# A delta-net stage: weight tiles split at unit five of the preceding tile, raw weights given out two tiles ahead

## The chip, the core and the metric

The kernel runs on one core of a Trainium2 chip. Its time is the device time of one execution in microseconds (us); the time of a kernel is the median of several runs. Five engines work side by side, each through its own queue in order: TensorE (PE in the profile, with its weight loads as PEld) multiplies matrices, VectorE (DVE), ScalarE (ACT) and GpSimd (POOL) work elementwise, SyncE (SP) issues most of the DMA transfers here. They wait for one another by semaphores.

## The reference, cut to what matters

A sequence of 1024 tokens with 1024 features goes through two residual layers. The first is a gated delta net (chunks of 64 in the reference, heads of 128) and a convolutional feed-forward part, the second a banded attention with another feed-forward part. All of it is float32. The stage that matters here is the delta net:

```python
proj = xn @ w_in                                  # 1024 x 4112
qkv = silu(causal_dwconv(proj[..., :3072], conv_w))
z = proj[..., 3072:4096]
q, k = l2norm(q) * 128 ** -0.5, l2norm(k)
o = chunk_gated_delta_rule(q, k, v, beta, g)      # a recurrence over chunks, 8 heads
o = rmsnorm(o, out_norm_w) * silu(z)
h = x + o @ w_out
```

## The kernel before

**Products in two halves.** Every float32 matrix product is made from rounded parts: an activation is split into `xh` (rounded) and `xl` (the rest), a weight tile into `whi` and `wlo`. `dense` (line 114) issues three matmuls for each of the eight k-slices: `whi` by `xh` (L120), `whi` by `xl` (L121), `wlo` by `xh` (L122). One such triple of 128 x 512 matmuls is called a unit here.

**Weight tiles.** The input projection has 32 weight tiles of 1024 x 128: eight each for k, q, v and the gate z. A tile has 16 units: eight for the first half of the sequence (half 0), eight for the second (half 1), each half ending in `post`. The raw tile (512 KB) is loaded by SP into `wraw` (L575; two buffers), cast on ScalarE to `whi` (L103, 128 x 1024) and subtracted on GpSimd in four pieces to `wlo` (L105, 128 x 256 each). `whi` and `wlo` have two buffers each. A generator `dense_tile` has these steps: issue the load, yield, split, yield, then the units. The last two z tiles share a generator `last_tiles`, which issues both loads at once and runs half 0 of both before half 1. After the input projection come 16 tiles of the output projection (`out_tile`, eight units each, loads on L1249).

**What follows a half tile.** `project.post` takes the accumulator through ScalarE (L615, L617), three VectorE taps of the short convolution (L625), a tanh on ScalarE (L630) and two GpSimd operations (L631, L632). For half 0 of k and q the result stays in `kq` and TensorE reads it there (L660 transposes q, L717 multiplies k by itself); the results of half 1 of k and q and both halves of v are stored to DRAM (line 635) and fetched later. The recurrence itself (`gram`, `invert_blocks`, `merge`, `prep`, `chain`, `output`, `finish`) is made of many short matmuls of 128 columns or fewer between operations of VectorE and ScalarE, and its loads and stores all go through SP: `at` (L748), `eq` (L750), `vv` (L766), the stores of d_m, d_u, d_e, d_y, d_z.

**What sets the order.** `Flow` is a planner that runs while the program is being written. It keeps a planned time `T`: a unit costs 0.69 us (line 292), each recurrence step has a fixed cost, and `on` keeps the planned busy time of VectorE, ScalarE and GpSimd. `run` emits the recurrence step of the highest rank whose inputs are due, else the next unit. The order thus written is binding for TensorE, VectorE and ScalarE (`manual_schedule`, line 1305). The order on GpSimd's and SP's queues is made afterwards, instruction by instruction, from what is ready first.

**The queue of tiles in the planner.** `nxt` holds tiles whose load has been emitted: one, or two when `brief` is set (line 262). From a tile's second unit on, `_dense` calls `fetch` after each unit (line 294). `fetch` first fills `nxt`, which emits loads, and then emits the split of the first entry, if the current tile has reached `split_at` units and six planned microseconds have passed since that entry's load was emitted (line 268). `split_at` comes with the current tile: 8, or what its generator yields after its split (26 in `last_tiles`, 1 in `out_tile`). `brief` is set in `last_tiles`, so the output tiles run with two entries. The six lines:

```python
while len(self.nxt) < (2 if self.brief else 1):
    ...
    self.nxt.append([e[2], 1, self.T, e[1], 8])
if split and self.nxt and self.nxt[0][1] == 1 and (split > 1 or self.T >= self.nxt[0][2] + 6.0):
    self.nxt[0][1] = 2
    self.nxt[0][4] = next(self.nxt[0][0]) or 8
```

A second `Flow` plans the attention stage (line 1973), with its own `brief` at line 2313.

Of the kernel before, what the change touches and what calls it, by code (L numbers as in the profile page):

```python
# [28 lines left out]
def trunk_kernel(  # L29
# [52 lines left out]
    def act_tiles(halves=(0, 1), into=None):  # L82

        xh, xl = into or ([[None, None] for _ in range(KT)], [[None, None] for _ in range(KT)])
        for k in range(KT):
            for s in halves:
                xh[k][s] = actp.tile([P, HALF], F32R, name=f"xh{k}_{s}", tag=f"xh{k}_{s}")
                xl[k][s] = actp.tile([P, HALF], F32R, name=f"xl{k}_{s}", tag=f"xl{k}_{s}")
        return xh, xl
# [39 lines left out]
    class Weave:  # L129
# [3 lines left out]
        def __init__(self):  # L133
            self.dense, self.short, self.solve, self.late = deque(), deque(), deque(), deque()
            self.now, self.credit, self.turn, self.budget = 0, 0.0, 0.0, 0.0
            self.at = {}
# [63 lines left out]
    class Flow(Weave):  # L200
# [4 lines left out]
        def __init__(self):  # L205
            super().__init__()
            self.T, self.free, self.aux = 0.0, dict(D=0.0, A=0.0, G=0.0), deque([[0.0], [0.0]])
            self.time, self.items, self.last, self.stalls = {}, [], 0, []
            self.auto, self.tick, self.slack, self.cur, self.nxt, self.units = True, 0, 0.5, None, deque(), 0
            self.brief, self.split_at, self.hold = False, 8, None  # L210

        def mark(self, key, t=None):
            super().mark(key)
# [46 lines left out]
        def fetch(self, split):  # L260

            while len(self.nxt) < (2 if self.brief else 1):
                e = self.pick()
                if e is None:
                    break
                next(e[2])
                self.nxt.append([e[2], 1, self.T, e[1], 8])
            if split and self.nxt and self.nxt[0][1] == 1 and (split > 1 or self.T >= self.nxt[0][2] + 6.0):
                self.nxt[0][1] = 2
                self.nxt[0][4] = next(self.nxt[0][0]) or 8  # L270

        def _dense(self):
            if self.cur is None:
# [128 lines left out]
    wv = None  # L402
# [107 lines left out]
    with ExitStack() as ph:  # L510
# [48 lines left out]
        def units(s, wt, post):  # L559

            ps = pacc.tile([P, HALF], F32, name="acc", tag="acc", bufs=3)
            for i in range(KT):
                dense(ps, wt, 0, xh, xl, FULL[i : i + 1], s, first=i == 0, last=i == KT - 1)
                if i < KT - 1:
                    yield
            post(s, ps)
            tiles[s] += 1
            if tiles[s] == 30:
                act_tiles((s,), acts)
                wv.mark(("acts", s))  # L570
            yield

        def raw_tile(c0):
            raw = wp.tile([P, KT, P], F32, name="wraw", tag="wraw", bufs=2)
            nc.sync.dma_start(out=raw, in_=a_w_in[:, c0 : c0 + P].rearrange("(k p) m -> p k m", p=P))  # L575
            return raw

        def split_tile(raw):
            wt = split_w(raw, [P, KT, P])
            wv.on("G", 2.75, wv.on("A", 1.0))  # L580
            return wt

        def dense_tile(c0, post):

            raw = raw_tile(c0)
            yield
            wt = split_tile(raw)
            yield
            for s in range(2):
                yield from units(s, wt, post)  # L590

        def last_tiles(jobs):

            raws = [raw_tile(c0) for c0, _ in jobs]
            yield
            wts = [split_tile(raws[0])]
            yield 26
            wv.brief = True
            for s in range(2):
                for n, (_, post) in enumerate(jobs):  # L600
                    for i, _ in enumerate(units(s, wts[n], post)):
                        yield
                        if s + n + i == 0:
                            wts.append(split_tile(raws[1]))
# [72 lines left out]
        def gram(t):  # L677
# [11 lines left out]
            def decay(i):  # L689
# [7 lines left out]
                yield wv.on("A", 1.45)  # L697

            fetch(hds[0])
            fetch(hds[1])  # L700
            yield wv.T + 5.5
            for i, hd in enumerate(hds):
# [7 lines left out]
                if i < 2:  # L710
                    fetch(hds[i + 2])
# [358 lines left out]
        def gate_z(hd):  # L1070
            def post(s, ps):
                zt = dp.tile([P, HALF], F32, name="zt", tag="zt", bufs=3)
                nc.scalar.copy(zt, ps)
                nc.sync.dma_start(out=d_z[hd][s], in_=zt)
                wv.mark(("z", hd, s), wv.on("A", 0.6) + 3.0)

            return 3072 + hd * P, post
# [86 lines left out]
        def begin_input():  # L1164

            warm = dp.tile([P, 2], F32, name="warm", tag="rsx", bufs=4)
            nc.scalar.activation(warm[:, 0:1], epst, AF.Sqrt)
            for i in range(4):
                take_x(i)
            for i in range(4):  # L1170
                norm_x(i)
            wts = [load_w(a_w_in, m * P) for m in (8, 9)]
            for i in range(4, 8):
                take_x(i)
            for s in range(2):
                if s == 1:
                    for i in range(4, 8):
                        norm_x(i)
                it = turn_x(s)
                for _ in range(3):  # L1180
                    next(it)
                for n, (wt, post) in enumerate(zip(wts, posts)):
                    ps = pacc.tile([P, HALF], F32, name="acc", tag="acc", bufs=3)
                    for i in range(KT):
                        dense(ps, wt, 0, xh, xl, FULL[i : i + 1], s, first=i == 0, last=i == KT - 1)
                        next(it, None)
                        if n == s == 1 and i in (1, 6):
                            next(g_it)
                    post(s, ps)
                    if n == s == 1:  # L1190
                        break
                    if n + s == 0:
                        w16, gT = load_gates()
                    if n + s == 1:
                        project_gates(w16, gT, s)
                    if n == 0 and s == 1:
                        g_it = gates(gT)
            wv.T, wv.free = 0.0, dict.fromkeys(wv.free, 0.0)
            for hd in range(2):
                for s in range(2):  # L1200
                    wv.mark(("k", hd, s), 3.0 * hd * s)
            wv.add(0, "gates", lambda: 0.0, g_it)
# [3 lines left out]
        def new_kq(hd):  # L1206
            kqs[hd, 0] = dp.tile([P, 2, HALF + 4], F32, name="kq", tag="kq", bufs=8)
            return kqs[hd, 0][:, 0]
# [77 lines left out]
        env["cut"] = 4  # L1286
        ORDER = [(w[0], int(w[1])) for w in "k0 k1 k2 k3 q0 q1 k4 q2 q3 k5 v0 v1 k6 v2 v3 k7 q4 q5 q6 q7 v4 v5 v6 v7".split()]
        wv = Flow()
        with tc.manual_schedule(engines={mybir.EngineType.PE}):
            for w, hd in ORDER:  # L1290
                if w == "k":
                    project(8 + hd, (lambda hd=hd: new_kq(hd), new_u), ("k", hd), {1: d_kq[hd][0]}, 1)
                elif w == "q":
                    project(hd, (lambda hd=hd: kqs[hd, 0][:, 1], new_u), ("q", hd), {1: d_kq[hd][1]}, 1)
                else:
                    project(16 + hd, (new_u, new_u), ("v", hd), d_v[hd])
            for hd in range(6):
                wv.dense.append((lambda: True, lambda: True, dense_tile(*gate_z(hd))))
            wv.dense.append((lambda: True, lambda: True, last_tiles([gate_z(hd) for hd in (6, 7)])))
            xh, xl = act_tiles()  # L1300
            begin_input()
            wv.fetch(0)
            wv.fetch(2)
# [651 lines left out]
    with ExitStack() as ph:  # L1955
# [17 lines left out]
        wv = Flow()  # L1973
# [540 lines left out]
```

## Time and profile before

| what | value |
|---|---|
| median of 3 runs | 2580.16 us (2577.23 to 2582.45) |
| profiled execution | 2574.87 us |
| its span, first to last instruction | 2572.9 us |
| granted TensorE clock, mean | 0.997 |
| TensorE matmuls, busy | 2499.4 us (97%) |
| VectorE, ScalarE, GpSimd busy | 1841.5, 1407.6, 1498.7 us (72, 55, 58%) |
| delta-net stage, from TensorE's first units to the last output tile | about 15 to 665 us |

The profile is that of one execution. A row of a group gives the source line, the engine, the operation, what it writes and reads, its count, its busy time in us and the mean in ns, and the engine's idle time ahead of it with what ended it. A row of the timeline gives the start in us, the duration in us, engine, line and operation, and in brackets the idle time ahead of it. A row of waits says which instruction of which engine waited for which, in us, with the number of times and the longest. Matmuls are pipelined and their ends are modelled: 128 x 512 matmuls are shown with some 0.39 us each, and start 0.23 us apart.

### The profile page before, as it was taken

Reading aid. Unit: us, or ns where it says so; the run is one execution under the profiler, and the core shown is the slowest. Engines: PE = TensorE matmul, PEld = TensorE weight load, DVE = VectorE, ACT = ScalarE, POOL = GpSimd, SP = SyncE. Lnnn points to the kernel's source line nnn. Section 1 sums busy time; section 2 is a strip of 40 time slices with the busy share of each in tenths; the row PEclk is TensorE's granted clock in tenths of the full one; section 3 lists DMA queues with packets and bytes.
Section 4 is the critical chain, followed back from the end, with each engine's and each line's share of the span. In section 5 each row is a group of like instructions: output and inputs, shape, how many; then the busy total and the mean of one; then the engine's idle time right before and its main releaser. Section 6 shows DMA issues by size and latency. Waiting matters only on the chain. (4 is left out here: it accounts for less than half of the span.)

```text
span 2572.9 us, 39308 instructions
## 1 busy us (share of the span) xinstructions
PE 2499.4 (97%) x13933; PEld 2071.4 (81%) x13933; DVE 1841.5 (72%) x2974; ACT 1407.6 (55%) x2708; POOL 1498.7 (58%) x1517
## 2 busy tenths in 40 slices
PE   7999999999999999999999999999999999999988
PEld 5878788888777888888778888888876788888877
DVE  5765775454588888888876656666478788888875
ACT  6444555464455555656545555656455555565553
POOL 3655554245447777777726444454443777777771
PEclk9999999999999999999999999999999999999999
DMA  4534445455336777777851111122432576777785
GB/s 128 138 103 121 119 120 165 130 174 167 107 82 137 149 145 152 154 154 154 166 177 41 56 43 48 61 63 71 140 105 82 140 153 143 154 154 150 157 191 176
DMA packets 317061, 325.93 MB, mean 127 GB/s; under 512 B 32832, under 2 KB 240960, under 8 KB 316864
## 3 DMA queue, kind: packets, MB, share of 16 engines
q1 hardware_dynamic: 285728, 219.33, 28.8%
q0 software_dynamic: 26240, 95.43, 20.8%
q10 hardware_dynamic: 4896, 8.65, 1.0%
q8 instruction: 110, 1.80, 0.3%
q14 instruction: 87, 0.71, 0.1%
HBM read 180.68 MB, written 142.67 MB: 126 GB/s over the span
## 5 line engine op out<-in xcount | busy, mean ns | idle before, releaser
L1362 POOL TENSOR_TENSOR ul<-r,uh 128x512 fp32r<-128x512 f32 x282 | 446.3, 1603 | 295.5 <-ACT uh L1383 280.4
L105 POOL TENSOR_TENSOR wlo<-wraw,whi 128x256 fp32r<-128x256 f32 (+3 forms) x338 | 249.9, 770 | 232.0 <-ACT whi L103 194.5
L120 PE MATMUL acc<-xh,whi 128*128 128x512 f32 x896 | 376.1, 420 | 0.3 <-ACT xh L1101 0.2
L122 PE MATMUL acc<-xh,wlo 128*128 128x512 f32 x896 | 352.6, 394 | 3.2 <-POOL wlo L105 3.2
L121 PE MATMUL acc<-xl,whi 128*128 128x512 f32 x896 | 352.9, 394 | 1.0 <-DVE xl L1102 0.6
L1383 ACT CAST uh<-r 128x512 fp32r<-128x512 f32 x296 | 181.8, 623 | 220.8 <-DVE r L1362 166.7
L1395 PE MATMUL pu<-xh,uh 128*128 128x512 f32 x552 | 216.2, 392 | 4.7 <-ACT uh L1383 1.8
L1397 PE MATMUL pu<-xh,ul 128*128 128x512 f32 x552 | 216.4, 392 | 4.2 <-POOL ul L1362 4.1
L1396 PE MATMUL pu<-xl,uh 128*128 128x512 f32 x552 | 215.6, 391 | 1.0 <-POOL xl L383 1.0
L1716 ACT COPY stage<-pd 128x1024 f32<-128x1024 f32 x180 | 175.1, 1014 | 49.7 <-PE pd L1397 45.8
L122 PEld LDWEIGHTS acc<-xh,wlo 128*128 128x128 f32 x896 | 168.5, 188 | 41.4 <-POOL wlo L105 4.0
L121 PEld LDWEIGHTS acc<-xl,whi 128*128 128x128 f32 x896 | 169.8, 189 | 27.1 <-DVE xl L1102 2.5
L120 PEld LDWEIGHTS acc<-xh,whi 128*128 128x128 f32 x896 | 169.5, 189 | 24.4 <-ACT xh L1101 1.2
L1490 DVE SCALAR_TENSOR_TENSOR val<-vpre,colt,val 128x1023 f32<-128x1023 f32 (+2 forms) x92 | 153.6, 1670 | 38.6 <-ACT val L1487 38.4
L2126 POOL TENSOR_SCALAR sS<-sS,st 128x640 f32<-128x640 f32 (+4 forms) x128 | 86.1, 677 | 159.9 <-DVE st L2124 146.0
L1362 POOL TENSOR_TENSOR dl<-a,dh 128x512 fp32r<-128x512 f32 x90 | 155.0, 1722 | 38.4 <-ACT dh L1383 37.1
L1490 DVE SCALAR_TENSOR_TENSOR gate<-gpre,colt,gate 128x1023 f32<-128x1023 f32 (+2 forms) x92 | 175.4, 1907 | 0.8
L2116 DVE CUSTOM_DVE_ANT_0 sS<-sc,bt 128x640 f32<-128x640 f32 (+4 forms) x128 | 84.1, 657 | 120.5 <-PE sc L2112 93.9
L1362 DVE TENSOR_TENSOR r<-r,r 128x512 f32<-128x512 f32 x168 | 132.0, 786 | 31.2 <-POOL ul L1362 29.8
L1397 PEld LDWEIGHTS pu<-xh,ul 128*128 128x128 f32 x552 | 103.9, 188 | 29.4 <-POOL ul L1362 7.8
L1395 PEld LDWEIGHTS pu<-xh,uh 128*128 128x128 f32 x552 | 103.8, 188 | 27.3 <-ACT uh L1383 2.3
L1396 PEld LDWEIGHTS pu<-xl,uh 128*128 128x128 f32 x552 | 103.9, 188 | 23.4 <-POOL xl L383 2.1
(389 smaller groups left out, 7063.7 us busy)
## 6 DMA issues: line engine op xcount, KB each, us to landing
r<-in_f_w_up_dram SPq DMA_DIRECT2D x172, 256.0 KB, 4.3
d_r<-stage POOLq DMA_DIRECT2D x78, 512.0 KB, 7.7
d_c<-stage POOLq DMA_DIRECT2D x70, 512.0 KB, 8.0
a<-in_f_w_down_dram SPq DMA_DIRECT2D x72, 256.0 KB, 2.8
wraw<-in_a_w_in_dram SPq DMA_DIRECT2D x32, 512.0 KB, 4.6
d_e<-stage POOLq DMA_DIRECT2D x32, 512.0 KB, 8.8
wraw<-in_a_w_out_dram SPq DMA_DIRECT2D x16, 512.0 KB, 4.1
d_r<-h ACTq DMA_DIRECT2D x32, 256.0 KB, 3.5
```

The lines of the kernel that those rows point to most:

```text
L105: nc.gpsimd.tensor_tensor(lo[:, c], raw[:, c], hi[:, c].bitcast(F32), op=ALU.subtract)
L120: mm(ps, hi[:, kw, wcol : wcol + P], rh[k][s], start=st, stop=False)
L121: mm(ps, hi[:, kw, wcol : wcol + P], rl[k][s], start=False, stop=False)
L122: mm(ps, lo[:, kw, wcol : wcol + P], rh[k][s], start=False, stop=sp)
L1362: tt = lambda eng, o, a, b, op: eng.tensor_tensor(o, a, b, op=op)
L1383: copy(hi, src)
L1395: mm(ps, w[0][:, cw], x[0], start=first, stop=False, skip_group_check=True)
L1396: mm(ps, w[0][:, cw], x[1], start=False, stop=False, skip_group_check=True)
L1397: mm(ps, w[1][:, cw], x[0], start=False, stop=last, skip_group_check=True)
L1490: nc.vector.scalar_tensor_tensor(t_[:, a:c1], p_[:, a - step : c1 - step], w[:, 2 - step : 3 - step], t_[:, a:c1], op0=ALU.mult, op1=ALU.add)
L1716: nc.scalar.copy(t_, ps)
L2126: nc.gpsimd.tensor_scalar(S, S, st[:, 3:4], 1.0, op0=ALU.mult, op1=ALU.mult)
```

## The change

The distance at which `_dense` lets `fetch` split the next tile becomes a field of the planner, `early`, 8 as before unless it is set. The delta-net stage sets it to 5, and sets `brief` at the start of the stage in place of in `last_tiles`. The attention stage keeps 8 and its own place of `brief`. No instruction of the engines is added or taken away; the planner's positions of the loads and splits change, and with them what it plans after each.

```diff
-            self.brief, self.split_at, self.hold = False, 8, None
+            self.brief, self.early, self.split_at, self.hold = False, 8, 8, None
...
-                self.nxt.append([e[2], 1, self.T, e[1], 8])
+                self.nxt.append([e[2], 1, self.T, e[1], self.early])
...
-                self.nxt[0][4] = next(self.nxt[0][0]) or 8
+                self.nxt[0][4] = next(self.nxt[0][0]) or self.early
...
             wts = [split_tile(raws[0])]
             yield 26
-            wv.brief = True
...
         wv = Flow()
+        wv.brief, wv.early = True, 5
```

## The prediction

> **What bounds the kernel now.** I first read the busy time by stretches of the delta-net stage, 15 to 665 us (columns: stretch, its length, busy time of TensorE's matmuls, of its weight loads, of VectorE, ScalarE and GpSimd with instruction counts, granted clock, share of the DMA engines, GB/s).
>
> ```profile
> core 0: us, PE busy (x) PEld busy (x) DVE busy (x) ACT busy (x) POOL busy (x), PEclk, DMA share, GB/s
> 15.00:140.00 125.00, 123.90 (x590) 98.17 (x590) 88.39 (x208) 64.77 (x142) 65.25 (x88) 1.00 0.41 111
> 140.00:310.00 170.00, 163.41 (x1273) 135.89 (x1271) 108.16 (x283) 81.24 (x221) 92.85 (x126) 1.00 0.40 115
> 310.00:400.00 90.00, 89.24 (x924) 75.08 (x925) 59.19 (x175) 47.50 (x143) 50.70 (x73) 1.00 0.49 134
> 400.00:500.00 100.00, 95.73 (x1009) 83.06 (x1007) 54.92 (x190) 54.08 (x180) 33.55 (x49) 1.00 0.49 145
> 500.00:565.00 65.00, 64.93 (x795) 55.50 (x796) 31.07 (x66) 38.82 (x104) 24.50 (x30) 0.97 0.53 159
> 565.00:665.00 100.00, 100.00 (x519) 84.38 (x518) 44.35 (x85) 45.96 (x95) 61.83 (x74) 1.00 0.58 174
> ```
>
> TensorE bounds every stretch: it is idle for 650 - 637.2 = 12.8 us of the 650, and the change adds or takes no matmul. GpSimd, the busiest of those that the change touches, has over a third of its time free. So the change can gain or lose only in TensorE's waits. The second view is who TensorE waited for in this stage (total us, times, longest).
>
> ```profile
> PE acc L122 <- POOL wlo L105: 3.2, 1, 3.2
> PE pv L783 <- DMA vv<-d_v: 3.1, 1, 3.1
> PE pq L660 <- POOL kq L632: 2.5, 1, 2.5
> PE pc L935 <- DVE vv L785: 1.5, 1, 1.5
> PE pc L935 <- DVE vv L933: 1.1, 1, 1.1
> ```
>
> These five come to 11.4 us, 0.44% of the kernel: that is about all the change could win. One of the five is the split itself. A measurement of this kernel can tell about 0.2%, 5.2 us, from no change.
>
> **Raw weights two tiles ahead: costed at nothing.** The plan emits the loads a tile earlier, but the order on SP's queue is made by readiness, and what holds a raw load is its buffer, of which there are two. The rows are one split's GpSimd half, the load that SP issued next, and SP's total wait of such loads.
>
> ```profile
> 75.64 2.84 POOL L105 TENSOR_TENSOR wlo<-wraw,whi 128x256 fp32r<-128x256 f32 x4 [1.24 <-ACT whi L103]
> ```
> ```profile
> 78.51 0.38 SPq L575 DMA_DIRECT2D wraw<-in_a_w_in_dram  x1
> ```
> ```profile
> SPq L575 <- POOL wlo L105: 71.2, 27, 6.4
> ```
>
> The split ends at 78.48 and the next load leaves at 78.51: on the chip the raw weights already run as far ahead as two buffers allow, and will after the change. The number of loads stays too. What hides this step is that the buffer, not the plan, is the limit; without that the step would move SP's order, which is the slower rival below. In the plan the earlier load has one effect: line 268 demands six planned microseconds between load and split. Now the load is given out at unit 2 (1.4 us at 0.69 a unit), so the split waits until 7.4, unit 11 of a tile without other work, whatever `split_at` says. With the load a tile earlier the test is always met, and unit 5 holds.
>
> **The split at unit 5: the same instructions, earlier.** One ScalarE cast and four GpSimd subtractions a tile, as before; they move on two queues, ScalarE's (in the plan's order) and GpSimd's (by readiness). How late they are now, for the three tiles that matter: the count of L120 matmuls, one a unit, from the start of the preceding tile to the cast (columns as above, only TensorE and its weight loads).
>
> ```profile
> 127.10:136.53 9.43, 5.16 (x13) 2.32 (x13) 1.00 0.27 83
> 295.30:304.88 9.58, 5.33 (x14) 2.48 (x14) 1.00 0.64 195
> 474.60:484.28 9.68, 3.98 (x9) 1.59 (x9) 1.00 0.63 203
> ```
>
> They came at units 13, 14 and 9 of 16. The second tile is the one that TensorE waited for:
>
> ```profile
> 305.86 2.06 POOL L980 TENSOR_TENSOR vv<-vv,rr 128x512 f32<-128x512 f32 x2 [5.03 <-DVE rr L551]
> 307.89 0.62 POOL L631 TENSOR_SCALAR th<-th 128x512 f32<-128x512 f32 x1
> 308.59 1.27 POOL L632 TENSOR_TENSOR u<-u,th 128x512 f32<-128x512 f32 x1
> 309.82 2.80 POOL L105 TENSOR_TENSOR wlo<-wraw,whi 128x256 fp32r<-128x256 f32 x4
> ```
> ```profile
> 310.60 0.50 PE L122 MATMUL acc<-xh,wlo 128*128 128x512 f32 x1 [3.22 <-POOL wlo L105]
> ```
>
> The cast at 304.88 was done a microsecond later, but GpSimd had just begun 4 us of other work. Nine units earlier is 9 x 0.69 = 6.2 us: the cast starts near 298.7 and the subtraction falls into the 5.03 us in which GpSimd stood idle before 305.86, done by about 304, over 3 us before its use at 307.4. Term A: -3.2, with little doubt, since every split is given out 3 to 9 units earlier than now, 2.1 us or more.
>
> **What was queued behind the late split.** The wait on kq, 147 us (GpSimd, ScalarE, TensorE):
>
> ```profile
> 136.71 0.63 POOL L631 TENSOR_SCALAR th<-th 128x512 f32<-128x512 f32 x1 [7.32 <-DVE B L808]
> 137.42 1.48 POOL L632 TENSOR_TENSOR u<-u,th 128x512 f32<-128x512 f32 x1
> 138.86 2.83 POOL L105 TENSOR_TENSOR wlo<-wraw,whi 128x256 fp32r<-128x256 f32 x4
> 143.56 1.27 POOL L734 COPY cm<-mn 32x128 f32<-32x128 f32 x4 [1.88 <-DVE mn L729]
> 144.93 0.62 POOL L631 TENSOR_SCALAR th<-th 128x512 f32<-128x512 f32 x1
> 145.63 1.26 POOL L632 TENSOR_TENSOR kq<-kq,th 128x512 f32<-128x512 f32 x1
> ```
> ```profile
> 140.50 0.63 ACT L630 ACTIVATE th<-kq 128x512 f32<-128x512 f32 x1
> ```
> ```profile
> 146.95 0.66 PE L660 MATMUL pq<-ident,kq 128*128 128x128 f32 x4 [2.52 <-POOL kq L632]
> ```
>
> The tanh for kq was ready at 141.13, with GpSimd in the split until 141.69; then it took the cm copies first, and stood 1.88 us for their input with kq's product behind them. Eight units (5.5 us) earlier the split lies in the 7.32 us of idle time before 136.71, GpSimd is free at 141.13 and kq is done near 143.1, ahead of the 144.4 at which TensorE asked. Bounds: 0 (cm stays in front) to -2.5; I take -2.5, term C, because kq's input was ready 2.4 us before that of cm and readiness makes this queue. In general the split moves away from the silu of half 0, which TensorE reads at once, to that of half 1, which goes through DRAM first (lines 634 and 766) and can be late by 2.8 us unnoticed. On ScalarE the cast comes to stand ahead of the tanh of half 1, with the same cover; if that cover is gone, the price is one subtraction set, 2.8 us a tile.
>
> The wait on vv, 500 us, starts on SP's queue:
>
> ```profile
> 491.80 0.38 SPq L575 DMA_DIRECT2D wraw<-in_a_w_in_dram  x1
> 492.29 0.52 SPq L813 DMA_DIRECT2D d_u<-W  x1
> 492.90 0.38 SPq L1074 DMA_DIRECT2D d_z<-zt  x1
> 493.37 0.47 SPq L766 DMA_DIRECT2D vv<-d_v  x1
> ```
> ```profile
> 500.07 1.01 PE L783 MATMUL pv<-ident,vv 128*128 128x128 f32 x4 [3.12 <-DMA vv<-d_v]
> ```
> ```profile
> wraw<-in_a_w_in_dram SPq DMA_DIRECT2D x28, 512.0 KB, 4.3
> ```
> ```profile
> vv<-d_v SPq DMA_DIRECT2D x16, 256.0 KB, 2.9
> ```
>
> SP had stood 6.4 us (the longest of its wait row above) on the raw load at 491.80; then four transfers left within 1.6 us, and vv took 500.0 - 493.4 = 6.6 us instead of its median 2.9. In the third row above nine units took 9.68 us, so four units less (9 to 5) is 4.3 us: the raw buffer comes free near 487.5, the 512 KB are in (4.3 us) when vv leaves, and vv lands near 496.5, before the 496.9 at which TensorE asked. Term B: bounds 0 and -3.1; I take -3.1, as vv's median is 3.7 under what it took. The Trainium skill, page "DMA: Bandwidth & Descriptors", section "Two DMAs through the same engine are not ordered", says that descriptors of one queue on one DMA engine start in the order of the queue. By that rule vv's lateness is the raw load's place ahead of it, and the sum below stands at -7.3; were vv slow by itself, the sum would be -4.2. The trace agrees with the rule here (6.6 against 2.9 us), and the same rule speaks for the slower rival.
>
> **What is late next.** The new places shift ScalarE's and GpSimd's times in the plan, so from 46 us on TensorE's order is laid anew and draws waits of its own. They are not in the trace: from 0 up to a set like the other three (-3.1 and -2.5 not won, and 1.5 + 1.1 more). I take +1.5, one wait of the size of the row on vv L785. Changes between short and long matmuls cost too:
>
> ```profile
> L120 PE MATMUL acc<-xh,whi 128*128 128x512 f32 x512 | 218.6, 427 | 0.3 <-ACT xh L1101 0.2
> L122 PE MATMUL acc<-xh,wlo 128*128 128x512 f32 x512 | 201.8, 394 | 3.2 <-POOL wlo L105 3.2
> ```
>
> The first matmul of a unit is longer by 33 ns on average, 512 x 0.033 = 17 us in all; a tenth more or fewer changes moves 1.7 us either way. I take 0.
>
> **Sum.** -3.2 - 3.1 - 2.5 + 1.5 = -7.3 us. The profiled execution took 2574.87, so it would take 2567.6; it lies 5.3 under the median of the runs, and the median goes from 2580.16 to 2572.9, 0.28% faster.
>
> **The rivals.** (1) Only the split's own wait goes, and the new order draws as many others as it loses: -3.2, 2577.0, within 0.2%. For it: four of the five waits are single events with other names than the split. Against it: two of them have the split right ahead of them in a queue. That the change does not do what it says is half true already (the loads) and ends here too.
> (2) Slower: the raw load as the blocker of SP's queue. The plan now offers SP each raw load a tile earlier. Where SP's order takes it up before the stores and loads around it, SP stands on the buffer with vv or at behind it, as it did before 491.80, and TensorE pays 3.1 us each time. For it: SP spent 71.2 us in 27 such waits. Against it: 26 of the 27 cost TensorE nothing, and earlier splits shorten them. It decides from three such events on: -3.2 + 3 x 3.1 = +6.1, 2586.3; four give +9.2, 2589.4.
>
> **How the numbers follow.** My forecast (A and at least one of B and C won): 0.45, with its own range 2568 to 2575. Rival 1: 0.29. Rival 2: 0.26, high for one known event in 27, because every wait of the new order that I can't see ends there. The low end: all 11.4 us of waits gone, 1.7 fewer changes, and 2.9 (lowest run 2577.23 against the median) of scatter: 2564. The high end takes in four events of rival 2: 2590. Faster 0.45, same 0.29, slower 0.26.
>
> **What would show it.** The cast of each tile stands at unit 5 to 7 of the tile before, not 8 to 14, and the split ends 2 to 6 us earlier against the tile's start. TensorE's wait table has no row on wlo between 15 and 665 us (A), none on kq L632 (C), none or a smaller one on vv<-d_v (B); raw loads still leave within 0.1 us of a split's end. The stage's idle time falls from 12.8 to about 5.5 us. I am wrong if TensorE gets new rows on DMA transfers, if SP's waits on wlo grow, or if the split at its new place holds up a silu that TensorE reads.

## The result, and the profile after

The changed kernel took 2570.91 us (median of 12 runs, 2566.82 to 2575.04), the kernel before, beside it, 2578.32 (12 runs, 2575.68 to 2587.15): a ratio of 0.9969, 95% interval 0.996 to 0.9978. That is 7.4 us less, against a forecast of 7.3. The size came out; most of the reasons did not.

The first view is TensorE's wait table of the delta-net stage, 15 to 665 us, of the changed kernel (total us, times, longest). Line numbers from 598 to 1287 are one lower than before: L659 is the old L660, L782 the old L783.

```profile
PE po L989 <- DVE mn L728: 3.4, 1, 3.4
PE pm L849 <- DVE T L845: 1.4, 1, 1.4
PE pv L782 <- DMA vv<-d_v: 1.0, 1, 1.0
PE acc L121 <- DVE xl L1101: 0.6, 2, 0.3
PE pc L930 <- DVE S L949: 0.6, 1, 0.6
PE pq L659 <- DMA kq<-d_kq: 0.3, 1, 0.3
```

The waits on wlo and on kq from GpSimd are gone. The row on vv is 1.0 us in place of 3.1; it is another wait, after 530 us, and the one at 500 us is gone. New ones stand in their places, the longest 3.4 us on a VectorE chain. The busy times by stretch (columns as in the prediction, a sum at the end):

```profile
140.00:310.00 170.00, 165.20 (x1288) 139.05 (x1288) 116.31 (x299) 81.83 (x216) 94.40 (x130) 0.99 0.40 117
310.00:400.00 90.00, 89.68 (x908) 74.93 (x908) 56.75 (x161) 51.74 (x167) 44.82 (x63) 0.98 0.43 121
400.00:500.00 100.00, 99.29 (x1035) 86.42 (x1034) 54.09 (x192) 51.97 (x167) 37.92 (x56) 1.00 0.50 151
500.00:565.00 65.00, 64.03 (x793) 54.32 (x792) 31.82 (x65) 42.18 (x107) 26.61 (x31) 1.00 0.63 192
565.00:665.00 100.00, 99.87 (x518) 84.12 (x517) 45.10 (x85) 41.77 (x90) 58.47 (x73) 1.00 0.53 155
sum 650.00, PE 642.12 PEld 537.57 DVE 388.04 ACT 333.08 POOL 327.69; mean PE 107.02 PEld 89.59 DVE 64.67 ACT 55.51 POOL 54.62
```

TensorE is idle for 7.9 us of the 650, before for 12.8. The granted clock is under 1 in two rows in which it was 1 before, of which more below. The splits moved as planned. The next rows count L120 matmuls, one a unit, from a tile's start to the cast for the next tile, for two tiles; then come one split's end and the next raw load (GpSimd, SP):

```profile
80.10:82.80 2.70, 1.56 (x4) 0.75 (x4) 1.00 0.52 152
292.20:294.70 2.50, 1.56 (x4) 0.56 (x3) 1.00 0.99 285
```
```profile
84.98 2.82 POOL L105 TENSOR_TENSOR wlo<-wraw,whi 128x256 fp32r<-128x256 f32 x4
```
```profile
87.83 0.37 SPq L575 DMA_DIRECT2D wraw<-in_a_w_in_dram  x1
```

The second tile is the one that TensorE waited for before; its cast stood at unit 14 and stands at unit 4. That is even ahead of the plan's unit 5: ScalarE only keeps its order, and runs ahead of the planned time where nothing holds it. The raw load still leaves 0.03 us after a split's end.

The profiled execution of the changed kernel has the same span, 2572.9 us, as that of before. It is one of the slower of its 12 runs (2574.72), with a mean granted clock of 0.993 against 0.997 before: its trace shows 33.5 us at a clock of 0.50, that of before 17.9, and half of the difference is 7.8 us, so the equal spans say little. The stage itself ended earlier: the first matmul of the feed-forward part starts at 667.0 us, before at 671.3.

### The profile page after: what moved, and what is told of

It reads as the page before. It is cut to its first block, busy times and chain, and to the rows that moved or that the text cites. A ratio compares the mean times of both kernels' runs of the same rounds, so it can differ in the third digit from the quotient of the medians.

```text
span 2572.9 us, 39314 instructions
## 1 busy us (share of the span) xinstructions
PE 2506.5 (97%) x13933; PEld 2079.2 (81%) x13933; DVE 1841.6 (72%) x2974; ACT 1407.0 (55%) x2708; POOL 1494.2 (58%) x1517
## 5 line engine op out<-in xcount | busy, mean ns | idle before, releaser
L120 PE MATMUL acc<-xh,whi 128*128 128x512 f32 x896 | 376.0, 420 | 0.1
L120 PEld LDWEIGHTS acc<-xh,whi 128*128 128x128 f32 x896 | 170.1, 190 | 24.7 <-ACT xh L1100 1.0
```

Source lines behind the costliest of these rows:

```text
L120: mm(ps, hi[:, kw, wcol : wcol + P], rh[k][s], start=st, stop=False)
```

## The experiments

Theory 1 was the prediction's: a late split stands ahead of other work in the queues of GpSimd and SP, and giving it out early takes three waits away. Theory 2: the order that the planner laid anew is what won.

**The split moved alone, with the old order.** The planner books a split where it did, but emits its instructions at unit 5, so TensorE and VectorE keep the old order instruction by instruction. The second run does so for three tiles only (the splits that stood ahead of the three waits), the third for all but these. The edit, with the condition of the second run:

```diff
+        def give(self, at):
+            if self.nxt and self.nxt[0][5] and self.units >= at:
+                self.nxt[0][5] = next(self.nxt[0][0])
...
                 self.fetch(self.units >= self.split_at)
+                self.give(5)
...
             raw = raw_tile(c0)
+            if c0 in (1664, 2560, 3712):
+                yield True
+                wt = split_w(raw, [P, KT, P])
+                yield
+                wv.on("G", 2.75, wv.on("A", 1.0))
```

> The order of TensorE and VectorE is word for word that of the kernel before; each split of the delta-net stage is given out at unit 5 of the preceding tile, and the planner still books it where it did. Theory 1 (the late split stood ahead of other work in the queues): the three waits of TensorE on wlo L105, on kq L632 at 147 us and on vv at 500 us go, 8.8 us, and nothing new comes, since the order is old: about 8.8 us under before, a ratio of 0.9966. Theory 2 (the new order that the planner laid is what won): only the wait on wlo goes, 3.2 us, ratio 0.9988, and the waits on kq and vv are still in the table with 2 to 3 us each.

> As the run with the old order and every split at unit 5, but only three tiles are split at unit 5: the sixth of k, the fifth of v and the sixth of z, whose splits stood ahead of the three waits; all others stay where they were. Theory 1: the same three waits go, 8.8 us, ratio 0.9966, as with all tiles. Theory 2: 3.2 us, ratio 0.9988.

> The complement: the old order, and all tiles but those three are split at unit 5. Theory 1: the three waits stay with 2 to 3 us each and the time stays that of before, ratio 1.000 within 0.1%. Theory 2 says the same of kq and vv, and the wait on wlo stays. A gain of 3 us or more would say that early splits help in a way that TensorE's wait table does not show.

Measured, as ratios to the kernel before: all tiles 0.9979 (0.997 to 0.9988), the three tiles 0.9982 (0.9971 to 0.9993), all but the three 1.0027 (1.0017 to 1.0037). The edit pushes the line numbers up by 12: L672 is the old L660, L795 the old L783. TensorE's waits with all tiles at unit 5 in the old order:

```profile
PE pq L672 <- POOL kq L644: 3.8, 1, 3.8
PE pc L947 <- DVE vv L797: 2.0, 1, 2.0
PE pc L943 <- issue: 0.7, 1, 0.7
PE acc L121 <- DVE xl L1114: 0.6, 2, 0.3
```

and with all but the three:

```profile
PE acc L122 <- POOL wlo L105: 5.5, 2, 5.0
PE pv L795 <- DMA vv<-d_v: 3.0, 1, 3.0
PE pq L672 <- POOL kq L644: 2.7, 1, 2.7
PE pc L947 <- DVE vv L797: 2.0, 1, 2.0
PE pc L943 <- issue: 1.1, 1, 1.1
```

Two of the three waits obey theory 1. Those on wlo and on vv are gone when their own splits are early and stay when only all the others are. For vv the queue shows it; SP in the run with all tiles early:

```profile
487.67 0.38 SPq L581 DMA_DIRECT2D wraw<-in_a_w_in_dram  x1
492.44 0.32 SPq L825 DMA_DIRECT2D d_u<-W  x1
492.91 0.32 SPq L1086 DMA_DIRECT2D d_z<-zt  x1
493.33 0.39 SPq L778 DMA_DIRECT2D vv<-d_v  x1
```

The raw load left at 487.67 in place of 491.80 (the prediction said near 487.5), vv left when it did before, now with the 512 KB out of its way, and TensorE has no wait on it. The third wait, on kq, does not obey: it grew from 2.5 to 3.8 us with the split out of its way, and to 4.6 us in the run with three tiles. So both theories' numbers missed (8.8 and 3.2 us; 5.4 measured by the ratio). The third run missed too: forecast unchanged, it lost 7.0 us by the ratio, 5.2 by the medians. Its waits on wlo, vv L797 and kq are 3 us longer than before (5.5, 2.0 and 2.7 against 3.2, 1.5 and 2.5), and its stage has three stretches of 3.4 us at half clock where that of before had one.

**The new order with a late split.** TensorE and VectorE in the order of the changed kernel, the planner booking at unit 5, and the split emitted at unit 11, or at 14:

```diff
                 self.fetch(self.units >= self.split_at)
+                self.give(11)      # the second run: 14
...
             raw = raw_tile(c0)
             yield
+            wv.on("G", 2.75, wv.on("A", 1.0))
+            yield True
+            wt = split_w(raw, [P, KT, P])
+            yield
```

> The order of TensorE and VectorE is word for word that of the changed kernel; the planner books each split at unit 5, but the split itself is given out at unit 11. Theory 1: one to three waits on wlo or on work behind the split come back, 3 to 9 us over the changed kernel, ratio to before 0.998 to 1.000. Theory 2: the new order carries the gain, the time stays within 1.5 us of the changed kernel, ratio to before 0.997.

> TensorE and VectorE in the order of the changed kernel word for word, every split given out at unit 14, as late as the one that TensorE waited for before. Theory 1: several waits on wlo come back, 3 us or more each: at least 6 us over the changed kernel, ratio to before 0.999 or more. Theory 2: the new order carries the gain whatever the split does, ratio 0.997.

Measured: 0.9966 (0.9953 to 0.9978) at unit 11, as theory 2 had it, and 1.001 (1.0 to 1.002) at unit 14, as theory 1 had it. The waits at unit 14:

```profile
PE pm L859 <- DVE T L855: 3.4, 1, 3.4
PE acc L122 <- POOL wlo L105: 2.6, 5, 1.2
PE po L999 <- POOL wlo L105: 2.3, 1, 2.3
PE pv L792 <- DMA vv<-d_v: 1.1, 1, 1.1
PE acc L120 <- ACT whi L103: 1.1, 2, 0.8
```

With the same order of TensorE, three units of 0.69 us decide 8.0 us of the stage by the profiles (the feed-forward part starts at 673.6 us in place of 665.6), and over 11 us of the kernel by the ratios: the place in the plan has a limit between units 11 and 14, and between unit 5 and unit 11 no difference is seen. So the gain needs no unit 5. It does not even need splits that stand earlier on average than before, as the count below shows.

**Each half of the change alone, and one unit more.**

```diff
-        wv.brief, wv.early = True, 5
+        wv.brief, wv.early = True, 8     # loads only
...
+        wv.early = 5                     # unit 5 only; brief set in last_tiles as before
...
+        wv.brief, wv.early = True, 4     # one unit earlier
```

> One half of the change alone: raw weights given out two tiles ahead all through the stage, splits at unit 8 as the field had it (without the six-microsecond test that now pushes them to units 8 to 14). The order is laid anew. Theory 1 (where a split stands among the queues): at unit 8 no split is as late as units 13 and 14, so the wait on wlo goes and the raw load ahead of vv leaves earlier: 5 us under before, ratio 0.998. Theory 2 (any newly laid order wins or loses by its own waits): anything from 0.996 to 1.004, and the wait table has other names than before.

> The other half alone: unit 5, but loads given out one tile ahead, so that the six-microsecond test still holds the split back to about unit 8 to 11. Theory 1: splits come little earlier than before where no recurrence work lies between, so most of the gain is lost: ratio 0.998 to 1.000. Theory 2: anything from 0.996 to 1.004.

> The change with unit 4 in place of 5: one unit is 0.69 us, so no split gains or loses by itself. Theory 1: the same waits as the changed kernel stay gone, ratio 0.997 within 0.1%. Theory 2: the order is laid anew once more and brings other waits, 0.994 to 1.002; a distance of over 3 us from the changed kernel is for theory 2.

Measured: loads only 0.9969 (0.996 to 0.9978), unit 5 only 0.9987 (0.9978 to 0.9995), unit 4 0.9979 (0.997 to 0.9988), a tenth of a percent behind the changed kernel with intervals that overlap, and too near to decide between the theories by its time. Unit 5 without the earlier loads leaves the six-microsecond test in force, and TensorE still waits for the split:

```profile
PE acc L122 <- POOL wlo L105: 4.5, 2, 3.2
PE pq L660 <- POOL kq L632: 2.8, 2, 2.7
PE acco L122 <- POOL wlo L105: 1.5, 1, 1.5
```

The loads alone bring all that the change brings, with splits that are on average no earlier. The table counts, as the prediction did, the unit of the preceding tile at which the cast starts in each profile, for the third to the thirtieth tile:

| kernel | unit, mean of 28 | latest | at 13 or later | ratio |
|---|---|---|---|---|
| before | 10.0 | 14 | 3 | 1 |
| changed | 4.8 | 10 | 0 | 0.9969 |
| old order, split at unit 5 | 4.5 | 8 | 0 | 0.9979 |
| new order, split at unit 11 | 10.6 | 14 | 2 | 0.9966 |
| new order, split at unit 14 | 13.0 | 16 | 20 | 1.001 |
| loads only | 9.9 | 13 | 1 | 0.9969 |
| unit 5 only | 9.6 | 15 | 3 | 0.9987 |

Each half of the change alone leaves the splits about where they were; only both together move them. Yet the loads alone, and the new order with the split at unit 11, have the whole gain with casts on average as late as before. One that mattered did move: the cast for the tile of the old wlo wait, the twenty-first, stands at unit 10 in both, not 14, so the 3.2 us of that row may still be the split's. For the rest, what they share with the changed kernel, and not with before, is an order of TensorE that the planner laid anew (with the loads alone from 201 us on) and raw loads given out earlier; the two were not separated. Early splits win something too (0.9979 in the old order), but add nothing to the new one. In the run with the loads alone the wait on vv is gone although vv left right behind its raw load (SP, then TensorE):

```profile
488.13 0.38 SPq L575 DMA_DIRECT2D wraw<-in_a_w_in_dram  x1
488.61 0.53 SPq L765 DMA_DIRECT2D vv<-d_v  x1
```
```profile
494.42 0.60 PE L782 MATMUL pv<-ident,vv 128*128 128x128 f32 x4
```

This vv took 5.4 us to land, at 494.0, and TensorE came to it only at 494.42, 5.8 us after it had left. In the kernel before TensorE asked 3.6 us after vv had left (496.95 against 493.37).

Unit 4 shows what theory 2 allows for and theory 1 does not, a wait on vv that came back (SP, then TensorE):

```profile
515.28 0.37 SPq L1248 DMA_DIRECT2D wraw<-in_a_w_out_dram  x1
519.29 0.82 SPq L765 DMA_DIRECT2D vv<-d_v  x1
```
```profile
525.52 1.09 PE L782 MATMUL pv<-ident,vv 128*128 128x128 f32 x4 [4.64 <-DMA vv<-d_v]
```

SP had stood on that raw load, 3.8 us of it for wlo; then the queue emptied in a burst, and vv took 6.1 us against a median of 4.4 in that run. That is the pattern of the prediction's slower rival, once. Its stage still started the feed-forward part at 665.2 us, 1.8 us ahead of the changed kernel's, so the profile does not show that this order is the worse one.

**The wait on kq.** In the old order GpSimd stood on the cm copies of the fifth head with the silu of kq behind them. The edit gives these copies out behind the silu, first with the old order and every split at unit 5, then with the loads alone:

```diff
+                    with tc.issue_after(silus["q", 3, 0]) if behind else ExitStack():
+                        for b in range(4):
+                            nc.gpsimd.tensor_copy(cm[r], mn[r, :, r])
...
+                if (hd, s) == (4, 0):
+                    wv.add(0.5, "cm", lambda: 0.0 if ("q", 3, 0) in wv.time else None, cms())
```

> The old order with every split at unit 5, and one thing more: on GpSimd the four cm copies of the fifth head, half 0, come behind the pending silu of the fourth q tile instead of ahead of it. No other queue changes by an instruction. If the cm copies ahead of kq were the cause of the wait on kq at 145 us, that wait (3.8 us without this edit) falls under 0.5 us, and with it the stretch at half clock that followed it: 4 to 5.5 us under the run without the edit, ratio to before 0.996. If the split or something else was the cause, the wait stays over 2 us and the ratio at 0.998.

> Loads given out two tiles ahead and splits at unit 8, with the same swap of cm copies and silu on GpSimd. TensorE waited 3.7 us on kq there, and a stretch of 3.4 us at half clock followed: if the swap takes both, 5.4 us less than without it, ratio to before 0.995, under the changed kernel too. If a new wait takes its place, ratio 0.997.

GpSimd's timeline without the edit (old order, splits at unit 5), and then with it:

```profile
139.06 1.49 POOL L644 TENSOR_TENSOR u<-u,th 128x512 f32<-128x512 f32 x1
144.93 1.28 POOL L746 COPY cm<-mn 32x128 f32<-32x128 f32 x4 [4.38 <-DVE mn L741]
146.30 0.62 POOL L643 TENSOR_SCALAR th<-th 128x512 f32<-128x512 f32 x1
147.00 1.26 POOL L644 TENSOR_TENSOR kq<-kq,th 128x512 f32<-128x512 f32 x1
```
```profile
143.09 0.62 POOL L643 TENSOR_SCALAR th<-th 128x512 f32<-128x512 f32 x1 [2.60 <-DVE ssk L735]
143.79 1.28 POOL L644 TENSOR_TENSOR kq<-kq,th 128x512 f32<-128x512 f32 x1
145.15 1.27 POOL L749 COPY cm<-mn 32x128 f32<-32x128 f32 x4
```

Without the edit GpSimd stood idle for 4.38 us on an input of cm while kq's could run. With it TensorE waited 0.7 us on kq in place of 3.8; the stretch at half clock behind it is gone, and the feed-forward part starts at 662.9 us in place of 667.9. The ratio was 0.9965 (0.9953 to 0.9976) against 0.9979 without; these intervals overlap, and the profiles decide. The cause of this wait is settled: a fixed order on GpSimd's queue, not the split. With the loads alone the same swap gave 0.9968 (0.9955 to 0.998), no gain over 0.9969: the wait on kq went, those on VectorE's T grew from 1.8 to 3.4 us, and the longest of them, 1.8 us, was followed by 3.4 us at half clock. No version beat the changed kernel beyond the intervals; five, the changed kernel among them, lie at 0.9965 to 0.9969.

**Waits put in.** In the profiles to this point TensorE's longer waits were mostly followed by a lower granted clock. To see whether the wait does it, seven waits were put into the last output tiles of the kernel before, where it has none; the added operations add zero:

```diff
             yield 1
+            if s == 1 and m > 0:
+                dw = dp.tile([P, HALF], F32, name="dw", tag="zt", bufs=3)
+                for _ in range((0, 1, 2, 4, 6, 8, 11, 14)[m]):
+                    nc.vector.tensor_scalar(dw, h[m - 1][:, hs(s)], 0.0, None, op0=ALU.mult)
+                nc.vector.tensor_tensor(xm[:, 0], xm[:, 0], dw[:, 0:P], op=ALU.add)
```

> The kernel before with waits put in: ahead of seven output tiles of half 1 TensorE waits for a chain of 1, 2, 4, 6, 8, 11 and 14 VectorE operations on the finished tile before it (they add zero). In the profiles so far a wait of 2.4 us or more of TensorE in this stage was followed in 12 of 16 cases by 3.4 us or 6.8 us at half clock. If the wait is what lowers the clock, the put-in waits of over 3 us are each followed within 4 us by such a stretch, and those under 2 us by none; the time grows by the waits and by 1.7 us for every stretch. If the stretches belong to other things, the last 100 us of the stage show none or one, wherever the waits lie.

One run took 2629.54 us, 49.8 over the median of before. TensorE's waits of the stretch, the matmuls around the shortest of them, and the busy times with the granted clock (the column after the counts) before and right after it:

```profile
PE acco L1262 <- issue: 28.4, 5, 7.9
PE acco L1262 <- DVE xm L1259: 5.7, 2, 3.0
```
```profile
632.04 0.40 PE L122 MATMUL acco<-xh,wlo 128*128 128x512 f32 x1
634.06 0.72 PE L1262 MATMUL acco<-ident,xm 128*128 128x128 f32 x4 [1.62 <-issue]
634.44 0.76 PE L120 MATMUL acco<-xh,whi 128*128 128x512 f32 x1
```
```profile
620.00:634.40 14.40, 12.78 (x65) 10.44 (x64) 4.60 (x9) 5.33 (x7) 5.91 (x9) 1.00 0.64 187
634.50:637.90 3.40, 3.40 (x14) 3.12 (x13) 0.10 (x1) 0.00 (x0) 0.00 (x0) 0.50 0.40 128
```

Behind each of the seven waits, from 2.0 to 3.9 us after its start, came 3.4 to 10.2 us at a clock of 0.50, behind the shortest (1.62 us) too, against the expectation. The waits sum to 34.1 us and leave 15.7 of the 49.8. The half clock outside the waits comes to about that: 44.4 us were granted, 13.8 of them while TensorE stood, and half of the other 30.5 is 15.3. So a wait put in lowers the clock, and costs more than its row says. This rests on one execution, and the VectorE operations that were added came with the waits.

## Why the prediction was right, point by point

The time came out, the way to it only in part, so the nearness of 7.3 and 7.4 is partly luck. The prediction counted the gain as that of earlier splits and entered the new order as a loss of 1.5 us. The runs showed that early splits in the old order win 5.4 us, and that a new order has the whole gain with splits on average as late as before (0.9966 at a mean unit of 10.6). At most 3.2 us of that can be the one split that TensorE had waited for, now at unit 10.

- **What bounds the kernel:** right. TensorE's idle time in the stage fell from 12.8 to 7.9 us; 5.5 had been forecast.
- **The loads, costed at nothing:** right for SP's queue (0.03 us from a split's end to the next load, before and after), wrong as a weight: this half alone gives the whole gain. The text gave it one effect in the plan, that the six-microsecond test no longer holds the split back. With the loads alone the casts hardly moved on average (9.9 against 10.0); what it changed besides is the order.
- **Term A, -3.2:** the mechanism is shown in the old order. The wait on wlo goes with its own split alone and stays without it. In the new orders a cast at unit 10 was early enough: no such wait with the loads alone, 0.8 us with the split at unit 11.
- **Term B, -3.1:** the mechanism is shown in the old order, with the raw load at 487.67 and no wait on vv. In the changed kernel the step was mis-sized: its new order has another wait on vv, 1.0 us, so the row fell by 2.1. The Trainium skill's rule on the order of a queue ("DMA: Bandwidth & Descriptors", "Two DMAs through the same engine are not ordered") is in keeping with the runs in the old order: vv left at the same time and landed in time once the 512 KB had gone ahead of it.
- **Term C, -2.5:** the row went, for another reason than the step gave. The step said that the split held kq back and that readiness would then put kq ahead of cm. With only the split moved, GpSimd still stood on cm and the wait grew to 3.8 us; the swap of cm and kq took it. In the changed kernel kq is ahead of cm because the order was laid anew.
- **New waits, +1.5:** too small. The rows that are new or grown (3.4, 1.4, 0.6, 0.3) less those that went (1.5, 1.1) make +3.1.
- **The sum:** the rows give -3.2 - 2.1 - 2.5 + 3.1 = -4.7, in keeping with 4.9 us less idle time and a stage that ends 4.3 us earlier. In these two executions half clock took more from the changed stage (6.8 us of it at 307 us, 1.0 of them within the wait, so 2.9 us lost, against 1.7 at 500 us before); without that its stage is 5.5 us shorter. Over all runs it is the other way: the mean granted clock of the 12 runs is 0.9958, that of 69 runs of the kernel before, taken beside the experiments, 0.9948. A thousandth of 2573 us is 2.6 us, an estimate, since the clocks stand in thousandths. With -4.7 this makes -7.3: the forecast won too much in waits and had no price for the clock, and the two errors cancel.
- **The slower rival** did not come in the changed kernel. One of its signs did: SP spent 77.9 us in 27 waits of raw loads on wlo against 71.2. But TensorE had one wait on a DMA of over half a microsecond. At unit 4 it came once, with 4.6 us on vv.

## What to carry to other kernels

When a planner gives work out by several tests, ask which test binds: a knob (unit 5) did next to nothing while a second condition held the work back. Then look where the work stands on the chip, and not only at the time: lifting that condition alone brought the whole gain and left most splits where they were, so the time alone would have credited the wrong cause. A wait named after an engine in the table is cured only when one has seen what stands in front in that engine's queue; move that one thing with all other orders kept, and see whether the row goes. Early enough is enough: with one order kept, units 5 and 11 tie, and between 11 and 14 lie 8.0 us of the stage.

## What the runs showed of the hardware

A wait of TensorE can cost more than its length. Seven of seven put-in waits, 1.6 to 7.9 us long, brought 3.4, 6.8 or 10.2 us at half clock, which by the count above is 1.4 to 3.0 us each on top. In the stage's natural waits of 2.3 us and more, over the profiles of the kernels before and after and eight of the runs above, 12 of 16 were followed by such a stretch, and no such stretch came there without such a wait ahead. In the run of the loads with the swap, which is not among the ten, a wait of 1.8 us was followed by one. The run-to-run scatter goes with it: the three fastest of the 12 runs of the changed kernel (2566.8 to 2568.2) have a mean clock of 0.997, the three slowest (2573.6 to 2575.0) 0.993 to 0.995. The Trainium skill, page "TensorE: Matmul & The Clock Gate", section "What's actually happening", tells of a free-running window of about 3.4 us and a return to half clock after an idle window; the lengths at half clock agree, but here a wait of 1.62 us, half a window, was enough. Why some waits of 2 to 3 us are not followed by one stays open. Length alone does not decide: the waits on kq and wlo of the kernel before (2.5 and 3.2 us) were not followed, the same two in the execution with waits put in (2.7 and 3.2 us) were. The place of the wait within such a window would explain it and was not tested.
